# A second attention stage on 192 keys a block: corners in quarters of TensorE, a shared middle of 128 keys, a shifted copy of the values, and reordered first loads

## The chip, the cores and the metric

One core of one Trainium2 chip runs the whole program. The metric is the device time of one execution in microseconds, as the median of several runs. Before the change three runs took 1920.82, 1922.53 and 1925.12 us, a median of 1922.53.

## The reference

Two layers are added to the residual stream x, 1024 tokens of 1024 features, all in float32:

```python
def reference(x, ...):
    for i in range(DEPTH):                                  # DEPTH = 2
        if i % N_MIXERS == 0:                               # layer 0
            h = rms_norm(x, conv_norm[j])
            x = x + short_conv_mixer(h, conv_w_in[j], conv_w[j], conv_w_out[j])
        else:                                               # layer 1
            h = rms_norm(x, attn_norm[j])
            x = x + dilated_attention_mixer(h, attn_w_in[j], ...)
    return x
```

The convolution mixer is `proj = h @ w_in` with 8192 columns split into four parts, `y = b * conv3(c * u) * silu(z)`, and `y @ w_out`. The attention mixer projects h on queries, keys and values of three groups of 16 heads of 64 features each, and on a gate z. Group g cuts the 1024 tokens into 1, 4 or 16 residue classes (dilations 1, 4, 16); within a class a query attends to itself and the keys before it within a window:

```python
logits = einsum('brhnqd,brhnkd->brhnqk', qs, kb) * HEAD_DIM ** -0.5   # blocks of 128 queries,
valid = (step >= 0) & (step <= span) & (key_pos >= 0)                # 256 keys: previous and own block
logits = where(valid, logits + bias, -inf)
lse = logsumexp(logits)
out = einsum('brhnqk,brhnkd->brhnqd', exp(logits - lse), vb)
```

The window spans 128 keys of the class (`span` = 128 in each group). So query a of a block needs the keys from a positions after the start of the previous block up to itself: 129 of the 256. The three groups' outputs of a head are mixed by a softmax of their `lse`, multiplied by `silu(z)` and projected with `w_out` (`y @ w_out`).

## The kernel before, in words

**First stage, to about 1590 us.** Layer 0 and the projections of layer 1 are matmuls of 1024 features. Each float32 operand is split into a high and a low part of the type fp32r, and a product takes three matmuls (high x high, high x low, low x high; lines 368 to 370). `load_x` (from line 162) loads the first half of x in eight tiles on SyncE's queue, scales each with the norm's gain into the high part on ScalarE (line 171) and takes the low part on VectorE (line 172). Behind the first tile it loads the first weight tile in two halves (`raw_w`, line 153), each split in the same way (`split_w`, lines 158 and 159), the halves behind the first and the second x tile. `products(0, 0)` then runs over the eight x tiles for one output tile of 128 features, three matmuls for each; `products(1, 0)` does the same for the next output tile with the second weight tile, after `load_consts` and `plain_w(0, 1, 2)`. From there the large products are run by Strassen's scheme (lines 264 to 307). The queries and keys are written to DRAM as `qkd`, the values as `vd`, the gate as `zd`, one slab for each pair of heads.

**Second stage, from about 1590 us.** There are 8 pairs of heads (`hp`) and 3 groups (`g`), so 24 units, run head by head, g = 0, 1, 2. `attention(hp, g)` makes each unit's steps: four of two blocks for g = 0 and 1, two for g = 2, whose classes are 64 tokens long, so that a step has four pairs of small blocks. That is ten steps a head and 80 in all. A block of 128 queries of g = 0 and 1 is either without a predecessor (the first block of a class: one in g = 0, four in g = 1, the first four of its order) and sees its own 128 keys, or has one and sees 256 in the layout, of which 192 are computed for each half of the queries. In g = 1 the first two steps hold only blocks without, the last two only blocks with predecessor. A step has these parts, on two heads s = 0, 1 at once (one on rows 0 to 63 of the array, one on 64 to 127):

- A: scores. Line 913 is for g = 2 (quarters of the array, 64 x 64), line 927 for a block without predecessor, line 932 for a block with one: for each half h of the queries a matmul of 192 columns into a part of the bank `ps` that is 256 columns wide. The 64 columns not written hold zeros. Then VectorE adds the bias `bt`, which also carries the mask, and takes the row's minimum of the negated sum, over 256 or 128 columns (line 945), into `xs` and `nl`. There are three banks `ps`.
- E: the exponential of `xs` on ScalarE, with its row sum (line 951).
- B: transposes of `xs` into the bank `pt`, one for each 128 columns of each head (line 958), and a copy of `pt` to `pts` by VectorE (line 869) or ScalarE (line 871); `copy` decides. There are two banks `pt`.
- C: products with the values `V` into the bank `po` (line 979 for g = 0 and 1, two for a block with predecessor, which add up in the bank; line 972 for g = 2). A bank holds half a unit's output, 64 features of two heads x 512 tokens. In g = 0 and 1 the first two steps fill one of the two banks and the last two the other, and each bank is copied to `O` as soon as its second step is done (`finish`, line 994; for g = 2 both at the unit's end, line 991).

Behind a head's last step follow, at fixed distances in steps, the shares of the three groups (through DRAM), the scaling of the outputs by them on VectorE (line 1048), their sum on GpSimd (line 1051), the gate and the split into high and low part.

**Order of the work.** The order is written out by hand: iteration k runs for lags 0, 1, LC = 4, 3, 5 to 16 and last LB = 2 what the step k minus the lag has put under that lag, then the exponentials of step k, then the dense work of iteration k. So A of step k comes first, then C of step k - 4, the head's scaling and the like, then B of step k - 2. The dense work is the output projection: for two heads and one tile of 128 features x 512 tokens, six matmuls into the bank `pd` (lines 1153 to 1155), which VectorE adds to `acc` at the start of the next iteration (line 1189). It starts in step 36, and the first of it is at about 1698 us. Loads are issued on SyncE's queue at fixed distances: queries and keys `qk` and the bias `bt` six steps ahead of a unit (lines 841, 886, 888), the values two steps ahead (line 850, two transfers). `V` has its 128 tokens of a block on the partitions; a partition's 1024 numbers are ordered by feature (64 of two heads), then by the eight blocks, so that the weights of one block are read with a stride of eight.

## Time and profile before

| | before |
|---|---|
| median of 3 runs | 1922.53 us (1920.82 to 1925.12) |
| profiled execution, its own time | 1922.75 us |
| its span in the trace | 1921.0 us |
| mean granted clock of TensorE | 0.996 |
| instructions in the trace | 30176 |
| bytes moved by DMA | 253.78 MB, mean 132 GB/s |
| share of SyncE's queue (q1) and of GpSimd's (q0) of 16 DMA engines' span | 28.5% and 12.3% |
| TensorE: lines 295, 297 and 298 (Strassen) on the chain that ended last | 22% each |
| TensorE: lines 979, 958 and 932 on it | 2%, 2% and 1% |

The table reads as follows. The span is what the profiler saw between the first and the last instruction, and the execution's own time is 1.75 us more. A granted clock of 1 is full speed. The chain that ended last is the work on which the end depended, followed back from the last instruction; most of it is the first stage. In the rows of a profile, PE is TensorE, PEld its weight loads, DVE is VectorE, ACT ScalarE, POOL GpSimd and SP SyncE, whose DMA queue is SPq. A matmul on float32 operands leaves two records in the trace, so that counts of the trace are twice those of the program for lines 913 to 932, 972 and 979, but not for a transpose or for fp32r.

### The profile page before, as it was taken

The page shows a single profiled execution, that of the slowest core. Times are in us where ns is not written, and L with a number is a line of the kernel's source. Part 1 is how long each engine was busy: PE and PEld are TensorE (multiplying, and loading weights), DVE is VectorE, ACT ScalarE, POOL GpSimd, SP SyncE. Part 2 cuts the span into 40 slices and gives each one's busy share as a digit, 9 for nine tenths or more (in the row PEclk, how much of TensorE's full clock was granted, in tenths as well). Part 3 has the DMA queues.
Part 4 walks back from the last instruction along what each step waited for, and adds up shares of the span by engine and source line. Part 5 has one row for each costly group of instructions (what it writes and reads, how often), then busy time and mean ns, then how long its engine had stood idle before and what let it go on. Part 6 is the DMA issues. An engine that isn't in the chain of part 4 may idle for free.

```text
span 1921.0 us, 30176 instructions
## 1 busy us (share of the span) xinstructions
PE 1891.1 (98%) x10690; PEld 1546.8 (81%) x10690; DVE 1488.1 (77%) x2802; ACT 881.0 (46%) x2013; POOL 910.4 (47%) x841
## 2 busy tenths in 40 slices
PE   8999999999999999999999999999999999999999
PEld 6888888888888788888888888888888887777777
DVE  7966666566666746698898698869898887988896
ACT  6533333333333534454334433444344438877780
POOL 0366666666666311334545554555454552343240
PEclk9999999999999999999999999999999999899999
DMA  6222223222222656423323332333233338897842
GB/s 207 93 81 88 91 76 106 88 88 83 88 82 89 224 179 223 152 83 132 110 98 116 116 110 89 126 110 115 80 118 103 117 126 278 256 285 222 231 137 89
DMA packets 117800, 253.78 MB, mean 132 GB/s; under 512 B 18494, under 2 KB 23838, under 8 KB 117648
## 3 DMA queue, kind: packets, MB, share of 16 engines
q1 hardware_dynamic: 93280, 176.89, 28.5%
q0 software_dynamic: 24368, 74.95, 12.3%
q8 instruction: 84, 1.38, 0.3%
q14 instruction: 68, 0.56, 0.1%
HBM read 192.53 MB, written 67.64 MB: 135 GB/s over the span
## 4 chain that ended last, share of the span: by engine, by line
PE 88%; DVE 4%; DMA 4%; issue 2%; POOL 1%; ACT 1%; SPq 0%; DVEq 0%; POOLq 0%; ACTq 0%
PE pp L295 22%; PE pp L297 22%; PE pp L298 22%; PE pp L550 3%; PE pp L551 3%; PE pp L549 3%; PE po L979 2%; PE pt L958 2%; DMA nld<-nl 1%; PE pp L370 1%; PE pp L369 1%; PE pp L368 1%; PE ps L932 1%; PE pd L1153 1%; PE pd L1155 1%
## 5 line engine op out<-in xcount | busy, mean ns | idle before, releaser
L159 DVE TENSOR_TENSOR ws<-wr,ws 128x512 fp32r<-128x512 f32 x283 | 296.1, 1048 | 116.6 <-ACT ws L158 115.5
L158 ACT ACTIVATE ws<-wr 128x512 fp32r<-128x512 f32 x283 | 177.8, 630 | 366.5 <-PE pp L298 239.6
L158 ACT ACTIVATE ws<-sr 128x512 fp32r<-128x512 f32 x276 | 173.3, 630 | 340.5 <-PE pp L298 277.2
L270 POOL TENSOR_TENSOR sr<-wr 128x512 f32<-128x512 f32 x138 | 197.2, 1429 | 249.7 <-DMA wr<-in_conv_w_in 112.8
L159 DVE TENSOR_TENSOR ws<-sr,ws 128x512 fp32r<-128x512 f32 x276 | 230.8, 842 | 85.0 <-ACT ws L158 83.0
L307 DVE TENSOR_TENSOR f<-pp,f 128x512 f32<-128x512 f32 x207 | 141.6, 684 | 80.4 <-PE pp L298 73.7
L951 ACT ACTIVATE xs<-xs,nl 128x256 f32<-128x256 f32 (+2 forms) x384 | 160.5, 423 | 0.3 <-DVE nl L945 0.3
L303 ACT ACTIVATE f<-pp 128x512 f32<-128x512 f32 x231 | 134.2, 581 | 4.9 <-PE pp L298 4.8
L270 POOL TENSOR_TENSOR sr<-wr,sr 128x512 f32<-128x512 f32 x69 | 90.6, 1313 | 64.5 <-issue 54.4
L945 DVE CUSTOM_DVE_ANT_0 xs<-ps,bt 128x256 f32<-128x256 f32 (+2 forms) x384 | 102.8, 325 | 12.1 <-PE ps L932 6.2
L295 PE MATMUL pp<-blkf,ws 128*128 128x512 f32 x276 | 109.8, 398 | 0.7 <-ACT f L303 0.7
L295 PE MATMUL pp<-blka,ws 128*128 128x512 f32 x276 | 107.5, 389 | 0.7 <-ACT f L303 0.7
L297 PE MATMUL pp<-blkd,ws 128*128 128x512 f32 x276 | 107.8, 391 | 0.0
L295 PE MATMUL pp<-blkd,ws 128*128 128x512 f32 x276 | 107.7, 390 | 0.0
L295 PE MATMUL pp<-blkb,ws 128*128 128x512 f32 x276 | 107.7, 390 | 0.0
L298 PE MATMUL pp<-blkf,ws 128*128 128x512 f32 x276 | 107.7, 390 | 0.0
L297 PE MATMUL pp<-blkf,ws 128*128 128x512 f32 x276 | 107.6, 390 | 0.0
L295 PE MATMUL pp<-blkg,ws 128*128 128x512 f32 x276 | 107.6, 390 | 0.0
L295 PE MATMUL pp<-blke,ws 128*128 128x512 f32 x276 | 107.6, 390 | 0.0
L298 PE MATMUL pp<-blke,ws 128*128 128x512 f32 x276 | 107.6, 390 | 0.0
L298 PE MATMUL pp<-blkb,ws 128*128 128x512 f32 x276 | 107.4, 389 | 0.0
L297 PE MATMUL pp<-blke,ws 128*128 128x512 f32 x276 | 107.4, 389 | 0.0
(339 smaller groups left out, 5180.1 us busy)
## 6 DMA issues: line engine op xcount, KB each, us to landing
wr<-in_conv_w_in SPq DMA_DIRECT2D x128, 256.0 KB, 3.2
wr<-in_wqk SPq DMA_DIRECT2D x96, 256.0 KB, 3.4
qkd<-blkc POOLq DMA_DIRECT2D x48, 512.0 KB, 3.9
qk<-qkd SPq DMA_DIRECT2D x48, 512.0 KB, 5.4
wr<-in_conv_w_out SPq DMA_DIRECT2D x64, 256.0 KB, 3.2
f<-in_x SPq DMA_DIRECT2D x48, 256.0 KB, 4.4
wr<-in_wv SPq DMA_DIRECT2D x48, 256.0 KB, 3.2
vd<-blkc POOLq DMA_DIRECT2D x96, 128.0 KB, 2.8
```

What stands on the lines that cost most here:

```text
L158: nc.scalar.activation(t[:, 0], src, AF.Copy)
L159: nc.vector.tensor_tensor(t[:, 1], src, t[:, 0].bitcast(F32), op=OP.subtract)
L270: nc.gpsimd.tensor_tensor(t, x, y, op=op)
L295: nc.tensor.matmul(ps, w[:, 0, ws], b[:, k, 0], start=new and k == 0, stop=False, skip_group_check=not new)
L297: nc.tensor.matmul(ps, w[:, 0, ws], b[:, k, 1], start=False, stop=False, skip_group_check=not new)
L298: nc.tensor.matmul(ps, w[:, 1, ws], b[:, k, 0], start=False, stop=end and k == 3, skip_group_check=not new)
L303: nc.scalar.activation(t, ps, AF.Copy)
L307: nc.vector.tensor_tensor(m, ps, m, op=OP.add)
L549: nc.tensor.matmul(ps[dt], w[:, 0, ws], b[:, k, 0], start=(q == k == 0), stop=False)
L550: nc.tensor.matmul(ps[dt], w[:, 0, ws], b[:, k, 1], start=False, stop=False)
L945: nc.vector.tensor_tensor_reduce(out=x, in0=flat[s][:, cols], in1=u["bt"][s][:, bs], op0=OP.add, op1=OP.min, scale=-1.0, scalar=3e38, accu ...
L951: nc.scalar.activation(x, x, AF.Exp, bias=nm, scale=-1.0, accum_out=L)
```

## The change

The change touches the start of the first stage and the second stage.

**First loads.** A copy of one column on ScalarE, which needs only a constant, is put at the start, so that the table of ScalarE's functions is loaded by it. `load_x` loads four half weight tiles between the first four x tiles, two of each of the first two weight tiles, and splits each behind its x tile. `first_products` runs over the x tiles once and does the three matmuls of both output tiles for each. The third weight tile's load comes ahead of the constants.

**Scores.** The 192 keys of a block with predecessor are laid out without a gap: columns 64 to 191 are the keys from 64 before the block's start to 63 after it, which both halves of the queries need (the shared middle), and columns 0 to 63 are the keys that one half needs alone, the corner: keys -128 to -65 for the lower half of the queries, 64 to 127 for the upper. `xs` and `pts` shrink to three times 128 columns. Reductions, exponentials and copies run over 192 columns. The bias is loaded in three pieces in this layout for each head.

**Corners and ends.** `corners` transposes the corners in quarters of the array (64 x 64 matmuls with `ident`), four for a block, two into each of the banks `pt`. B transposes only the middle, one for each head. `ends` multiplies the transposed corners with the values, four 64 x 64 matmuls for a block, into the same output columns as the middle's product. Two heads and two halves of the queries make the four quarters. C has one product of 128 keys for a block and head, the middle with `W`, or for a block without predecessor its own keys with `V`.

**W.** The values are loaded a second time for g = 0 and 1, shifted by 64 tokens, so that the middle's 128 keys stand on the 128 partitions: two more transfers for each such unit, behind V's, with two buffers. Corners are taken from `V` or `W`, whichever has them on the right rows.

**Steps and banks.** In g = 1 a step now has one block without and one with predecessor ([0, 4], [1, 5], [2, 6], [3, 7]). Both output banks of a unit are taken at its first corner products, and both are copied at its last step.

**Order.** An iteration runs A of step k, `corners` of step k - 2, `ends` of step k - 4, and then B of step k - 2 if the iteration has no dense work; then lags 1, 4 (C), 3, 5 to 16 as before; and B last if it has.

```diff
+    nc.scalar.activation(consts.tile([P, 1], F32, name="warm"), ones, AF.Copy)
...
-                if hf == kt == 0:
-                    r0 = raw_w(a["conv_w_in"][0, 0], 2)
+                if hf == 0 and kt < 4:
+                    k, c = ((0, 0), (1, 0), (0, 1), (1, 1))[kt]
+                    if kt < 2:
+                        raws[k] = wq.tile([P, 1024], F32, name="wr", tag="wr", bufs=2)
+                    cs = slice(c * HALF, c * HALF + HALF)
+                    nc.sync.dma_start(raws[k][:, cs], a["conv_w_in"][0, k][:, cs])
...
-                if hf == kt == 0:
-                    W[0] = [split_w(r0[:, :HALF])]
-                if hf == 0 and kt == 1:
-                    W[0].append(split_w(r0[:, HALF:]))
+                if hf == 0 and kt < 4:
+                    W.setdefault(k, []).append(split_w(raws[k][:, cs]))
...
+            def first_products():
+                t = [cps.tile([P, HALF], F32, name="pp", tag="pp") for _ in range(2)]
+                for kt in range(KT):
+                    ws = slice(kt % 4 * P, kt % 4 * P + P)
+                    for k in range(2):
+                        w, b = W[k][kt // 4], B[kt // 4, 0]
+                        nc.tensor.matmul(t[k], w[:, 0, ws], b[:, kt % 4, 0], start=(kt == 0), stop=False)
+                        nc.tensor.matmul(t[k], w[:, 0, ws], b[:, kt % 4, 1], start=False, stop=False)
+                        nc.tensor.matmul(t[k], w[:, 1, ws], b[:, kt % 4, 0], start=False, stop=(kt == KT - 1))
+                return t
...
+                plain_w(0, 2, 2)
                 load_consts()
-                plain_w(0, 1, 2)
-                plain_w(0, 2, 2)
-                ps[0, 0] = products(0, 0)
+                ps[0, 0], ps[1, 0] = first_products()
                 load_x(1)
-                ps[1, 0] = products(1, 0)
...
+            if g < 2:
+                t = WS[hp, g] = ap.tile([P, P + 1, 8], F32, name="W", tag="W", bufs=2)
+                t = t.rearrange("p a b -> p (a b)")
+                nc.sync.dma_start(t[:64, 1:S + 1], vd[hp, g, 64:])
+                nc.sync.dma_start(t[64:, :S], vd[hp, g, :64])
...
-                        nc.sync.dma_start(b0, rows[:, :256])
+                        nc.sync.dma_start(b0[lo], rows[:64, :256])
+                        nc.sync.dma_start(b0[up, 64:], rows[64:128, 64:256])
+                        nc.sync.dma_start(b0[up, :64], rows[64:128, 192:256])
...
+                        w = P if alone else 192
+                        for h, to, at_, m in ((0, 0, 0, 64), (1, 0, 0, P)) if alone else \
+                                ((0, 0, -P, 192), (1, 64, -64, P), (1, 0, 64, 64)):
+                            for s, hs in enumerate((lo, up)):
+                                nc.tensor.matmul(flat[s][64 * h:64 * h + 64, x0 + to:x0 + to + m],
+                                                 q[hs, b * P + 64 * h:b * P + 64 * h + 64],
+                                                 k[hs, b * P + at_:b * P + at_ + m], start=True, stop=True)
+                        todo.append((slice(x0, x0 + w), j, slice(128, 256) if alone else slice(0, 192)))
+                        c.append((x0, j, b, alone))
+                        x0 += w
...
+                def corners():
+                    if g == 2:
+                        return
+                    for s in range(2):
+                        pt.append(ptp.tile([P, 4, P], F32, name="pt", tag="pt"))
+                    n = 0
+                    for i, (x0, j, b, alone) in enumerate(c):
+                        if not alone:
+                            for h, hs in enumerate((lo, up)):
+                                for s in range(2):
+                                    x = xs[s].rearrange("p a b -> p (a b)")
+                                    to = (lo, up)[s ^ i]
+                                    nc.tensor.matmul(pt[h].rearrange("p a b -> p (a b)")
+                                                     [to, 256 + 64 * n:256 + 64 * n + 64],
+                                                     x[hs, x0:x0 + 64], ident[hs, hs], start=True, stop=True)
+                            n += 1
...
+                        for i in range(len(c)):
+                            x0 = i * P if g == 2 else c[i][0] + (0 if c[i][3] else 64)
+                            nc.tensor.transpose(pt[s][:, i], x[:, x0:x0 + P], ident)
+                        pts.append(ap.tile([P, 3, P], F32, name="pts", tag="pts", bufs=6))
+                        copy(*(y.rearrange("p a b -> p (a b)")[:, :n] for y in (pts[s], pt[s])), s)
...
+                def banks_for():
+                    if js[0] == 0:
+                        for q in range(2):
+                            u["po", q] = opp.tile([P, HALF], F32, name="po", tag="po")
+                def put(i, s, hs, j, qs, w, p):
+                    po = u["po", i][hs]
+                    po = po.rearrange("p (s c) -> p c s", c=4)[:, j % 4] if g == 1 else \
+                        po[:, P * (j // 2):P * (j // 2) + P]
+                    nc.tensor.matmul(po[:, qs], w, p, start=(i, s) in first, stop=True, skip_group_check=True)
+                    first.discard((i, s))
+                def ends():
+                    if g == 2:
+                        return
+                    banks_for()
+                    V = VS[hp, g]
+                    w = WS[hp, g].rearrange("p a b -> p (a b)")
+                    for h, qs in enumerate((lo, up)):
+                        n = 256
+                        for i, (x0, j, b, alone) in enumerate(c):
+                            if not alone:
+                                for s, hs in enumerate((lo, up)):
+                                    rs = (lo, up)[s ^ i]
+                                    p = pts[h].rearrange("p a b -> p (a b)")[rs, n:n + 64]
+                                    if h == s ^ i:
+                                        put(i, s, hs, j, qs, V[rs, hs, b - 1 + h], p)
+                                    else:
+                                        b0 = 512 * s + b + (1 if h else -1)
+                                        put(i, s, hs, j, qs, w[rs, b0:b0 + 505:8], p)
+                                n += 64
...
+                                put(i, s, hs, j, slice(0, P), (V if alone else WS[hp, g])[:, hs, b], pts[s][:, i])
+                    if js[-1] == 7:
+                        for q in range(2):
                             finish(q)
...
+                           [[2 * q, 2 * q + 4], [2 * q + 1, 2 * q + 5]] if g == 1 else
...
-            for lag in (0, 1, LC, 3, *range(LC + 1, 17), LB):
-                for f in steps[k - lag].get(lag, ()) if 0 <= k - lag < len(steps) else ():
+            lags = [(0, 0), ("corners", LB), ("ends", LC)] + [(x, x) for x in (1, LC, 3, *range(LC + 1, 17))]
+            lags.insert(len(lags) if extra.get(k) else 3, (LB, LB))
+            for what, lag in lags:
+                for f in steps[k - lag].get(what, ()) if 0 <= k - lag < len(steps) else ():
```

The order of instructions shows it at three places. The first is TensorE's order in steps 7 and 8 of the first head, where the products pass from unit g = 0 to g = 1. `ps` are scores, `xs` and `pts` the exponentials before and after the transpose, `pt` the bank between, `po` an output bank. Before:

```order
L932 MATMUL ps<-qk 64x192 x8
L979 MATMUL po<-pts,V 64x128 x8
L958 MATMUL pt<-ident,xs 128x128 x4
L913 MATMUL ps<-qk 64x64 x16
L979 MATMUL po<-pts,V 64x128 x4
L958 MATMUL pt<-ident,xs 128x128 x8
```

and now:

```order
L992 MATMUL pt<-ident,xs 128x128 x4
L1007 MATMUL po<-pts,W 64x128 x4
L934 MATMUL ps<-qk 64x64 x16
L979 MATMUL pt<-ident,xs 64x64 x4
L1007 MATMUL po<-pts,W 64x64
L1007 MATMUL po<-pts,V 64x64 x2
L1007 MATMUL po<-pts,W 64x64
L992 MATMUL pt<-ident,xs 128x128 x4
L1007 MATMUL po<-pts,V 64x128 x2
L1007 MATMUL po<-pts,W 64x128 x2
```

The transposes moved ahead of the products (line 958 stood last, line 992 stands ahead of line 1007's 64x128), and behind the scores of step 8 stand four small transposes and four corner products, which are the first to write the next unit's output banks.

The second is VectorE's order at the same place; `nl` are the row minima, `o` the unit's output. Before:

```order
L945 ISA xs,nl<-ps,bt 128x256
L945 ISA nl 128x1
L994 COPY o<-po 128x512
L869 COPY pts<-pt 128x256
L945 ISA xs,nl<-ps,bt 128x64
```

and now:

```order
L959 ISA xs,nl<-ps,bt 128x192
L959 ISA nl 128x1
L888 COPY pts<-pt 128x320
L1062 COPY o<-po 128x4x128 x2
L959 ISA xs,nl<-ps,bt 128x64
```

One copy of 512 columns stood ahead of the copy of transposed scores; now both halves of the output are copied there, one behind the other, after it.

The third is SyncE's order of issues around the loads of a head's second unit. Before:

```order
L888 DMA bt<-sk_85 128x256 x2
L841 DMA qk<-qkd 128x1024 x2
L850 DMA V<-vd 128x512 x2
L886 DMA bt<-sk_86 64x64 x4
L841 DMA qk<-qkd 128x1024 x2
```

and now:

```order
L907 DMA bt<-sk_87 64x256
L908 DMA bt<-sk_87 64x192
L909 DMA bt<-sk_87 64x64
L907 DMA bt<-sk_87 64x256
L908 DMA bt<-sk_87 64x192
L909 DMA bt<-sk_87 64x64
L855 DMA qk<-qkd 128x1024 x2
L864 DMA V<-vd 128x512 x2
L869 DMA W<-vd 64x1024
L870 DMA W<-vd 64x1024
L905 DMA bt<-sk_88 64x64 x4
```

Six bias pieces stand where two stood, and the two transfers of W follow V's.

74 lines of the change are left out of this document (28 added, 46 removed).

## The prediction

> **What bounds the kernel now.** I read the totals first, then the busy time by stage, then the order of work on TensorE in the second stage, then its waits.
>
> ```profile
> PE 1891.1 (98%) x10690; PEld 1546.8 (81%) x10690; DVE 1488.1 (77%) x2802; ACT 881.0 (46%) x2013; POOL 910.4 (47%) x841
> ```
>
> The windows give TensorE, its weight loads, VectorE, ScalarE and GpSimd, then the granted clock and the DMA share:
>
> ```profile
> 0.00:46.00 46.00, 38.22 (x166) 30.20 (x167) 31.70 (x60) 30.34 (x50) 2.50 (x11) 1.00 0.60 200
> 46.00:1588.00 1542.00, 1538.99 (x6790) 1265.65 (x6789) 1172.25 (x1665) 621.34 (x1059) 811.01 (x709) 1.00 0.35 112
> 1588.00:1698.00 110.00, 99.74 (x1396) 79.59 (x1395) 96.76 (x436) 95.25 (x386) 34.33 (x44) 0.94 0.85 274
> 1698.00:1880.00 182.00, 176.96 (x2142) 140.48 (x2140) 161.13 (x600) 132.79 (x519) 62.59 (x77) 0.99 0.69 205
> 1880.00:1921.00 41.00, 37.19 (x204) 30.86 (x203) 26.24 (x44) 1.26 (x2) 0.00 (x0) 1.00 0.28 103
> ```
>
> From 46 to 1588 us TensorE idles 3 us in 1542, and the change touches nothing there: whatever is won before 46 us arrives at 1588. What is left is the first 46 us (7.8 us idle) and the second stage, 333 us. Its 80 steps fall into two kinds. To 1698 us a step is attention alone; there TensorE is idle 10.3 us and its clock averages 0.94, while VectorE works 96.8 of 110 us. From 1698 us most steps carry six matmuls of the output projection, and TensorE works 177 of 182.
>
> The timeline of TensorE shows three groups a step; the time of a group is from its start to the next start:
>
> ```profile
> 1601.33 0.71 PE L927 MATMUL ps<-qk 64*128 64x128 f32 x8
> 1601.97 1.24 PE L979 MATMUL po<-pts,V 128*64 128x128 f32 x16
> 1603.15 1.09 PE L958 MATMUL pt<-ident,xs 128*128 128x128 f32 x8
> 1604.17 0.88 PE L932 MATMUL ps<-qk 64*64 64x192 f32 x16
> ...
> 1606.75 0.88 PE L932 MATMUL ps<-qk 64*64 64x192 f32 x16
> 1607.56 1.24 PE L979 MATMUL po<-pts,V 128*64 128x128 f32 x16
> 1608.73 0.66 PE L958 MATMUL pt<-ident,xs 128*128 128x128 f32 x4
> 1609.32 0.69 PE L913 MATMUL ps<-qk 64*64 64x64 f32 x32
> 1609.94 0.76 PE L979 MATMUL po<-pts,V 128*64 128x128 f32 x8
> 1610.63 1.09 PE L958 MATMUL pt<-ident,xs 128*128 128x128 f32 x8
> ...
> 1622.45 1.07 PE L972 MATMUL po<-pts,V 64*64 64x64 f32 x32
> 1623.45 1.09 PE L958 MATMUL pt<-ident,xs 128*128 128x128 f32 x8
> ```
>
> An fp32 matmul leaves two records, a transpose one. Scores of two blocks with predecessor (x16) take 0.81 us, their eight transposes 1.02 (from 1603.15 to 1604.17), their eight products with V 1.17: 3.00 us. Two blocks without predecessor take 0.64 (1601.33 to 1601.97) + 0.59 (four transposes) + 0.69 = 1.92 us. Differences of equal groups give the slopes: (1.17-0.69)/8 = 0.06 us a record of V products and 0.21 us fixed; (1.02-0.59)/4 = 0.107 us a transpose and 0.16 fixed. The fixed part is the turn from one array shape to the next. The quarter-array groups (64\*64) take 0.62 us for 32 records at L913, 0.014 each less 0.17 fixed; at L972, with weights taken from V at a stride, 1.00 us, 0.026 each. So four quarters do run at once: 16 matmuls of 64 columns in 0.62 us.
>
> **The first 46 us.** The first activation waits for x, and its table load only starts then (SP's issues, their row in the transfers of the first 8 us with the us to landing, then ScalarE and TensorE):
>
> ```profile
> 1.65 0.90 SPq L153 DMA_DIRECT2D wr<-in_conv_w_in  x2
> ...
> wr<-in_conv_w_in SPq DMA_DIRECT2D x2, 256.0 KB, 3.9
> ...
> 3.87 1.28 ACT L171 ACT_TABLE_LOAD   x1 [3.87 <-DMA f<-in_x]
> ...
> 5.79 0.61 ACT L158 ACTIVATE ws<-wr 128x512 fp32r<-128x512 f32 x1
> ...
> 6.46 0.79 PE L368 MATMUL pp<-blka,ws 128*128 128x512 f32 x1 [6.46 <-ACT ws L158]
> ...
> 14.21 0.50 PE L369 MATMUL pp<-blkb,ws 128*128 128x512 f32 x1 [0.56 <-DVE blkb L172]
> ...
> 20.27 0.39 PE L370 MATMUL pp<-blkb,ws 128*128 128x512 f32 x1
> ```
>
> With the table in place before x lands, ScalarE could be 1.28 us earlier, but the first weights then bind: their copy cannot start before they land, 1.65 + 3.9 = 5.55 us by the first rows, and it starts at 5.79 now. So TensorE starts some 0.3 us earlier, not 1.3. The larger gain is the interleaving: each x tile now feeds six matmuls (1.4 us) where it fed three, so TensorE no longer waits tile by tile, and the 48 matmuls that end at 20.5 us should end near 18.8. The loads behind them keep their order and gain the same. Term: -1.7 us, bounds -3 and 0 (the second weight comes late and the wait is only moved).
>
> **Steps of the second stage, on TensorE.** For two blocks with predecessor: scores as many columns in 12 instructions for 8, 0.81 to 0.83 us; corners 16 records at L913's 0.014, 0.22; four transposes 0.59; corner products 16 records at L972's 0.026, 0.42 (their V and W columns have V's stride); shared products 8 records, 0.48 + 0.21 = 0.69. Scores, corners and corner products share one array shape and pay one turn, so the turns stay three a step. Sum 2.75 against 3.00: -0.25, three times a head. The middle group now pairs a block without and one with predecessor: 0.73 + 0.11 + 0.59 + (0.21 to 0.42) + 0.69 = 2.33 to 2.54 us, against the mean of 1.92 and 3.00, 2.46: four times a head -0.13 to +0.08. The open size is the corner products on two of the four quarters: 0.21 if the strided read is shared by quarters, 0.42 if each pays its own; I take the middle. The first step of a head, -0.2. Per head about -0.8, for eight heads -6.5. In the 44 steps from 1698 us on it counts in full (-3.6); before, VectorE sets part of the pace, and I take half (-1.5). Term: -5.1, bounds -12 and +1.
>
> **Waits of TensorE there:**
>
> ```profile
> PE pt L958 <- DVE pts L869: 6.3, 7, 2.5
> PE po L979 <- DVE o L991: 4.1, 5, 0.9
> ...
> PE pd L1153 <- DVE acc L1189: 2.1, 1, 2.1
> PE ps L932 <- DVE nl L945: 1.1, 2, 0.7
> ```
>
> *Unit boundaries.* Both output banks are now held from a unit's first corner product to its last step, where both are copied one behind the other, and the next unit's corner products, early in the next step, wait for both; behind them on TensorE stand the transposes, the shared products and any dense matmuls, and VectorE and ScalarE wait for these.
>
> ```profile
> L994 DVE COPY o<-po 128x512 f32<-128x512 f32 x32 | 22.0, 686 | 2.9 <-PE po L979 2.7
> ...
> L991 DVE COPY o<-po 128x512 f32<-128x512 f32 x16 | 15.2, 1022 | 0.4 <-PE po L972 0.4
> ...
> L945 DVE CUSTOM_DVE_ANT_0 xs<-ps,bt 128x256 f32<-128x256 f32 x176 | 64.8, 419 | 6.2 <-PE ps L932 3.9 <-ACT xs L951 1.6
> ...
> L945 DVE CUSTOM_DVE_ANT_0 xs<-ps,bt 128x128 f32<-128x128 f32 x80 | 19.3, 286 | 4.3 <-PE ps L932 2.3 <-ACT xs L951 1.4 <-PE ps L927 0.5
> ```
>
> Two copies of the first and second group take 1.3 us, of the third 2.0; until then TensorE has scores and corners, 0.8 us. That is 0.5 us at the first boundary and 0.2 more than now at the third, in the 4.3 heads' worth of steps without dense work: 4.3 x 0.7 = 3.0. With dense matmuls (1.5 us) between, they cover it. Term: +3.2, bounds 0 and +17 (see the rival).
>
> *Relief of VectorE and ScalarE.* A score reduction of 192 columns instead of 256 saves half of (419-286) = 67 ns, 176 times, 11.7 us of VectorE; the copies shrink by a quarter. What TensorE can get of it is in its waits (13.6 us above) and the clock after them:
>
> ```profile
> 1650.05 3.80 DVE L1048 TENSOR_TENSOR o<-o,sqacc 128x1024 f32<-128x1024 f32 x1
> 1653.78 0.54 DVE L869 COPY pts<-pt 128x384 f32<-128x384 f32 x1
> ...
> 1654.38 0.66 PE L958 MATMUL pt<-ident,xs 128*128 128x128 f32 x4 [2.52 <-DVE pts L869]
> ...
> 1658.00:1668.00 10.00, 9.46 (x78) 7.34 (x75) 8.94 (x36) 7.98 (x23) 5.01 (x9) 0.62 0.56 182
> ```
>
> A copy of transposed scores stood behind a scaling of 3.80 us; TensorE lost 2.52 us and then ran ten at 0.62 clock, 3.8 us more. In steps without dense work the copy now comes ahead of such scaling; but the next score reductions then stand behind it, and VectorE's chain there is as long as before. Term: -3, bounds -10 and 0. [...]
>
> *Loads.* W adds 0.5 MB to each of 16 units, and the bias of a head comes in three pieces instead of one.
>
> ```profile
> 1589.87 0.84 SPq L850 DMA_DIRECT2D V<-vd  x2
> ...
> 1599.38 1.00 PE L979 MATMUL po<-pts,V 128*64 128x128 f32 x12
> ...
> V<-vd SPq DMA_DIRECT2D x48, 256.0 KB, 6.5
> ```
>
> W is issued behind V on SP's queue, after 4 more bias issues (0.42 us each, as V's), and needed by the first corner products, a little before 1599.38. By the 6.5 us of V, under a DMA share near 1, it lands about 1600: +0.7 once (0 to 3). Later units have V issued some five steps ahead. The DMA share of 0.85 to 1698 us rises by 4 MB in 30: +1, bounds 0 and +6.
>
> **Sum.** -1.7 - 5.1 + 3.2 - 3 + 0.7 + 1 = -4.9 us. The profiled execution took 1922.75 us, span 1921.0 with 1.75 around it, and is 0.2 above the median 1922.53. So 1917.9, rounded 1918.0. About 0.2% (3.8 us) is what a measurement of this kernel can tell from no change; the forecast is just beyond it.
>
> **Rivals.**
> *VectorE's late copies decide (slower), 0.15.* At every one of 24 unit boundaries TensorE waits 0.9 us, today's longest, or more, since VectorE is behind with reductions when the last step ends; dense matmuls don't cover it when VectorE is 1.5 us late. 24 x 0.9 = 21.6, less the 4.1 there are: +17.5 in place of +3.2, 1932. For it: VectorE works 161 of 182 us even in the dense steps. Against: it has 12 us less to do. It decides from about 0.4 us mean wait a boundary.
> *Quarters that share a bank run one after the other, 0.06.* The corner products of one block write both halves of one bank from different row quarters; at L913 and L972 the row quarters write different banks, so no row shows this. If serial, corner products double, 0.42 x 64 steps = 27 us more: 1945. [...] No run here shows it yet.
> *No change, 0.2.* The strided reads cost 0.42 in every step and VectorE's chain hides the rest: term two -1, relief 0, boundaries +3.2: about 1922.5.
> *A larger gain, 0.2.* The long waits at heads' ends shrink below what drops the clock, and the steps gain in full: relief -9, term two -7: 1910.
>
> The forecast has 0.39; its own range is 1914 to 1922, so some two fifths of it fall within 0.2%. Faster: 0.24 + 0.2 = 0.44; same: 0.15 + 0.17 of the third = 0.32; slower 0.24. The range 1908 to 1930 leaves out the bank rival, half of the first rival and the end of the last, under 0.2.
>
> **What would show it.** Right: 48 matmuls done by 19 us; second stage without dense 2 to 4 us shorter, with dense 3 to 5; a two-predecessor step of about 2.75 us; TensorE waiting for output copies 7 us in all. Wrong: corner products above 0.6 us a step (banks or strides), waits for output copies above 15 us, waits for W, or 48 matmuls still ending at 20 us.

## The result and the profile after

The changed kernel took 1941.64 us, the median of four runs (1939.88 to 1943.38), against 1923.61 us for the kernel before in four runs: the ratio is 1.0091, with a 95% interval of 1.0078 to 1.0104. By the ratio that is slower by 17.5 us (the two medians differ by 18.0), where the prediction said 4.6 us faster and put the end of its range at 1930. The profiled execution took 1943.38 us, its span is 1941.6.

The totals and the stages, first the busy times of the page, then the windows that answer to those shown before (TensorE, its weight loads, VectorE, ScalarE, GpSimd, granted clock, DMA share, GB/s); the window to 1711 us ends at the first dense matmul, the next at the last step's scores:

```profile
PE 1899.7 (98%) x12082; PEld 1563.7 (81%) x12082; DVE 1464.5 (75%) x2802; ACT 865.8 (45%) x2014; POOL 910.0 (47%) x841
...
0.00:46.00 46.00, 38.63 (x168) 31.19 (x169) 31.88 (x60) 31.06 (x51) 2.85 (x12) 1.00 0.62 202
...
1588.00:1711.00 123.00, 103.66 (x2041) 87.31 (x2039) 87.04 (x435) 89.47 (x385) 34.27 (x44) 0.88 0.95 263
1711.00:1882.00 171.00, 163.31 (x2684) 134.09 (x2684) 142.09 (x560) 115.71 (x486) 59.15 (x75) 0.99 0.92 254
1882.00:1942.00 60.00, 55.11 (x419) 45.27 (x408) 38.21 (x83) 9.34 (x36) 3.33 (x3) 0.96 0.19 72
```

VectorE works 87 us up to the first dense matmul where it worked 96.8, as the change meant, and TensorE is not the shorter for it: it idles 19 us there, at a clock of 0.88 instead of 0.94. The column that moved the other way is the next to last: the DMA engines are busy 0.95 and 0.92 of the time, where it was 0.85 up to 1698 us and 0.75 from there to the last step's scores at 1864 us. Taking the second stage from its first scores, to the first dense matmul, to the last scores, to the last matmul's end, the profiled executions compare like this:

| stretch | before, us | after, us | difference |
|---|---|---|---|
| up to the first scores | 1591.18 | 1590.53 | -0.65 |
| to the first dense matmul | 106.95 | 121.00 | +14.05 |
| to the last step's scores | 166.04 | 170.56 | +4.5 |
| to the end of the last matmul | 53.0 | 55.7 | +2.7 |

TensorE's waits in the second stage (what waited, for whom; us in total, times, longest; "issue" is time without a wait that the profile shows):

```profile
PE ps L947 <- DVE nl L959: 9.3, 6, 5.6
PE ps L947 <- issue: 4.2, 3, 2.1
PE pd L1223 <- DVE acc L1259: 4.2, 1, 4.2
...
PE po L1007 <- DMA W<-vd: 2.1, 2, 1.2
...
PE po L1039 <- DVE o L1060: 0.6, 1, 0.6
...
PE po L1007 <- DVE o L1057: 0.3, 1, 0.3
```

The wait for output copies, 4.1 us before, is nearly gone, and so is the one for copies of transposed scores (6.3). What replaces them are a few long waits for VectorE's score reductions and for an addition to `acc`. VectorE's own waits say why they come late:

```profile
DVE xs L959 <- PE ps L947: 15.7, 16, 1.5
DVE mx L1087 <- DMA ml<-nld: 10.1, 3, 7.1
...
DVE mx L1087 <- issue: 2.3, 1, 2.3
```

`ml` are the minima and sums of a head's first two groups, written to DRAM and fetched again by GpSimd's queue, and line 1087 is the first use of them for the shares. While VectorE stands there, the reductions of the next scores stand behind it: in the longest of these waits line 1087 starts at 1698.51 us, after 7.08 us of idle time, and the next reductions follow from 1700.26, though the last of their scores ended at about 1693.2. In the chain of waits one of these places reads as follows (start, us, what):

```profile
1669.70 5.18 DMA fd<-fo
...
1678.66 11.83 DMA nld<-nl
...
1691.31 7.08 DMA ml<-nld
...
1698.51 0.19 DVE mx L1087
```

A store of 16 KB was 11.83 us on its way and the fetch behind it 7.08, and TensorE at the same place:

```profile
1694.94 0.42 PE L947 MATMUL ps<-qk 64*64 64x64 f32 x2
1700.95 1.12 PE L947 MATMUL ps<-qk 64*64 64x64 f32 x14 [5.59 <-DVE nl L959]
```

These look like transfers that wait among others. In the transfers of the second stage up to 1865 us (KB each, median us from issue to landing) `ml` went from 4.8 to 7.1 us, `fb`, the shares fetched for the scaling, from 7.0 to 9.2:

```profile
W<-vd SPq DMA_DIRECT2D x32, 256.0 KB, 7.6
fb<-fd POOLq DMA_DIRECT2D x24, 256.0 KB, 9.2
...
ml<-nld POOLq DMA_DIRECT2D x28, 8.0 KB, 7.1
```

### The profile page after: what moved, and what is told of

Its sections match the earlier page's. It is cut to its first block, busy times and chain, and to the rows that moved or that the text cites. A ratio compares the mean times of both kernels' runs of the same rounds, so it can differ in the third digit from the quotient of the medians.

```text
span 1941.6 us, 33113 instructions
## 1 busy us (share of the span) xinstructions
PE 1899.7 (98%) x12082; PEld 1563.7 (81%) x12082; DVE 1464.5 (75%) x2802; ACT 865.8 (45%) x2014; POOL 910.0 (47%) x841
## 3 DMA queue, kind: packets, MB, share of 16 engines
q0 software_dynamic: 24368, 74.95, 11.9%
## 4 chain that ended last, share of the span: by engine, by line
PE 84%; DMA 5%; DVE 3%; issue 2%; POOL 1%; SPq 0%; ACT 0%; DVEq 0%; POOLq 0%
PE pp L299 22%; PE pp L301 21%; PE pp L302 21%; PE pp L564 3%; PE pp L565 3%; PE pp L563 3%; PE po L1007 2%; DMA nld<-nl 1%; PE pt L992 1%; DMA W<-vd 1%; PE ps L947 1%; PE pd L1223 1%; PE pd L1225 1%; PE pd L1224 1%; DMA ml<-nld 1%
## 5 line engine op out<-in xcount | busy, mean ns | idle before, releaser
L160 DVE TENSOR_TENSOR ws<-wr,ws 128x512 fp32r<-128x512 f32 x283 | 285.1, 1009 | 116.1 <-ACT ws L159 115.1
L965 ACT ACTIVATE xs<-xs,nl 128x192 f32<-128x192 f32 (+2 forms) x384 | 151.1, 399 | 2.1 <-DVE nl L959 2.1
L299 PE MATMUL pp<-blkf,ws 128*128 128x512 f32 x276 | 109.8, 398 | 0.7 <-ACT f L307 0.7
L959 DVE CUSTOM_DVE_ANT_0 xs<-ps,bt 128x192 f32<-128x192 f32 (+2 forms) x384 | 90.8, 295 | 22.5 <-PE ps L947 15.7
L299 PE MATMUL pp<-blkg,ws 128*128 128x512 f32 x276 | 107.6, 390 | 0.0
L302 PE MATMUL pp<-blkf,ws 128*128 128x512 f32 x276 | 107.4, 389 | 0.0
L302 PE MATMUL pp<-blkg,ws 128*128 128x512 f32 x276 | 107.4, 389 | 0.0
```

What stands on the lines that cost most here:

```text
L160: nc.vector.tensor_tensor(t[:, 1], src, t[:, 0].bitcast(F32), op=OP.subtract)
L299: nc.tensor.matmul(ps, w[:, 0, ws], b[:, k, 0], start=new and k == 0, stop=False, skip_group_check=not new)
L302: nc.tensor.matmul(ps, w[:, 1, ws], b[:, k, 0], start=False, stop=end and k == 3, skip_group_check=not new)
L959: nc.vector.tensor_tensor_reduce(out=x, in0=flat[s][:, cols], in1=u["bt"][s][:, bs], op0=OP.add, op1=OP.min, scale=-1.0, scalar=3e38, accu ...
L965: nc.scalar.activation(x, x, AF.Exp, bias=nm, scale=-1.0, accum_out=L)
```

## The experiments

The theory after this reading, D: W's transfers fill the DMA engines, the small transfers that carry the shares come late, and VectorE and TensorE wait behind them. The rivals were Q, that the quarters of the array cost TensorE more than they save, and O, that the new order or the output copies at a unit's end cost it. Fourteen kernels were run; the ratio is always to the kernel before, with the 95% interval.

| run | what it is | ratio | interval |
|---|---|---|---|
| the change | | 1.0091 | 1.0078 to 1.0104 |
| e1_no_w | without W's transfers | 1.0017 | 1.0006 to 1.0029 |
| e2_before_traffic | before, with W's bytes moved in DRAM | 1.0017 | 1.0006 to 1.0027 |
| e3_w_aligned | W not 4 bytes off | 1.0122 | 1.0102 to 1.0143 |
| e4_b_last | transposes always last | 1.0127 | 1.0109 to 1.0146 |
| e5_start_only | before, with the new first loads | 0.9987 | 0.9979 to 0.9995 |
| e6_late_weights | first use of `ml` later | 1.0113 | 1.0100 to 1.0126 |
| e7_w_v_form | W in V's form of transfer | 1.0064 | 1.0050 to 1.0078 |
| e8_no_w_dense_read | e1, corner weights without stride | 1.0010 | 0.9999 to 1.0020 |
| e9_no_w_whole_bias | e1, bias in one transfer | 1.0016 | 1.0006 to 1.0026 |
| e10_w_unread | W loaded, not read | 1.0122 | 1.0097 to 1.0147 |
| e11_w_on_gpsimd | W copied from V by GpSimd | 1.0107 | 1.0092 to 1.0122 |
| e12_w_on_act | W copied from V by ScalarE | 1.0065 | 1.0050 to 1.0080 |
| e13_start_and_order | before, new first loads and order | 0.9986 | 0.9976 to 0.9995 |
| e14_start_order_all | the same, order in every iteration | 1.0042 | 1.0029 to 1.0056 |

**Without W's transfers.**

```diff
-                t = WS[hp, g] = ap.tile([P, P + 1, 8], F32, name="W", tag="W", bufs=2)
-                t = t.rearrange("p a b -> p (a b)")
-                nc.sync.dma_start(t[:64, 1:S + 1], vd[hp, g, 64:])
-                nc.sync.dma_start(t[64:, :S], vd[hp, g, :64])
+                WS[hp, g] = VS[hp, g]
...
-                                        b0 = 512 * s + b + (1 if h else -1)
+                                        b0 = 512 * s + b
```

> The changed kernel without W's two transfers a unit; it reads V where it read W, so that its output is not the reference's. Theory D (the DMA engines are full: W and the bias pieces delay the small transfers of the shares, VectorE stands waiting for ml in program order, and TensorE idles and loses clock behind it): of the 18 us lost most comes back, 1920 to 1927 us, DMA share before the first dense step back from 0.96 to about 0.85, waits of VectorE for ml back from 12 us to under 4. Rival Q (scores, corners and corner products in quarters of the array cost TensorE more than they save): no more than 4 us come back, 1937 to 1942. Rival O (the order of transposes and the two output copies at a unit's end): the same, 1937 to 1942.

Measured: 1926.86 us, ratio 1.0017. Its windows, to the first dense matmul and to the last scores, and VectorE's wait for `ml`:

```profile
1588.00:1699.00 111.00, 100.91 (x2042) 85.06 (x2042) 85.92 (x434) 89.08 (x385) 36.44 (x49) 0.94 0.86 269
1699.00:1865.00 166.00, 161.12 (x2684) 132.44 (x2686) 141.77 (x559) 116.06 (x487) 55.38 (x69) 1.00 0.80 226
...
DVE mx L1084 <- DMA ml<-nld: 2.9, 1, 2.9
```

The DMA share falls back to 0.86, the clock returns to 0.94, the wait for `ml` from 10.1 to 2.9 us, and 0.74% (14 us) of the loss is gone: Q and O had it within 4 us of the changed kernel. W is the larger part. Not every transfer is early again: `ml` lands in 5.8 us here (7.1 with W, 4.8 before), but `fb` still takes 8.9 (9.2 and 7.0), so its lateness is not W's.

**W loaded, not read**, to tell its traffic from the wait for it.

```diff
-                    w = WS[hp, g].rearrange("p a b -> p (a b)")
+                    w = V.rearrange("p a b -> p (a b)")
...
-                                put(i, s, hs, j, slice(0, P), (V if alone else WS[hp, g])[:, hs, b], pts[s][:, i])
+                                put(i, s, hs, j, slice(0, P), V[:, hs, b], pts[s][:, i])
```

> The changed kernel with W loaded in full but read by nobody (products and corners read V, wrong values). If W costs by its traffic: 1938 to 1943, ratio 1.0075 to 1.010, as with W read. If it costs by the wait of the first corner products for it and by what stands behind that on TensorE: ratio 1.001 to 1.004, near the kernel without W's transfers.

Measured: ratio 1.0122, no faster than with W read, though nobody waits for W. So it is the traffic. But its way to the time is another here: VectorE has no wait for `ml`, which lands in 5.1 us, and TensorE's largest wait is for the queries and keys themselves:

```profile
PE ps L947 <- DMA qk<-qkd: 10.4, 4, 5.3
```

So the part of theory D that says which transfer is late does not hold in general; that W's traffic costs the time does.

**The same bytes on the kernel before.** The bytes go from `vd` to a place in DRAM (`more`) that nobody reads.

```diff
+        more = dram.tile([HP, 2, 2, 64, S], F32, name="more")
...
+            if g < 2:
+                for i in range(2):
+                    nc.sync.dma_start(more[hp, g, i], vd[hp, g, 64 * i:64 * i + 64])
```

> The kernel before plus W's bytes: behind V's transfers of each unit of the first two groups two transfers of 64 rows of 4 KB from vd to a place in DRAM that nobody reads. D: slower by 8 to 20 us, 1931 to 1943, with VectorE waiting for ml. Q and O: within 2 us of before, 1922 to 1926.

Measured: 1927.55 us, ratio 1.0017: slower by 3 us, not by 8 to 20. D as put here fell: the bytes alone do not cost what W costs. VectorE's wait for `ml` did rise, from 1.3 to 6.3 us in two places.

**The form of W's transfers.** The next run loads W as V is loaded, 128 rows of 2 KB a transfer instead of 64 rows of 4 KB.

```diff
-                nc.sync.dma_start(t[:64, 1:S + 1], vd[hp, g, 64:])
-                nc.sync.dma_start(t[64:, :S], vd[hp, g, :64])
+                for q in range(2):
+                    nc.sync.dma_start(t[:, half(q)], vd[hp, g, :, half(q)])
...
-                                        b0 = 512 * s + b + (1 if h else -1)
+                                        b0 = 512 * s + b
```

> The changed kernel with W loaded in the form of V: two transfers of 128 rows of 2 KB instead of two of 64 rows of 4 KB, not shifted (its products take wrong values, the work is the same). If it is the form (64 partitions at a time) that makes W dear, 47 us of 16 engines' time for 8.4 MB where V's form costs about half: DMA share before the first dense step falls from 0.96 to 0.91, and 6 to 12 us come back, 1930 to 1936. If it is the bytes: within 3 us of 1942.

Measured: ratio 1.0064, so 5 of the 17.5 us come back, a little less than the 6 to 12 of the first theory. The pages' rows for SyncE's queue (packets, MB, share of 16 engines' span) say what W took of the engines, for the changed kernel, without W, and in V's form:

```profile
q1 hardware_dynamic: 98912, 185.29, 30.7%
```

```profile
q1 hardware_dynamic: 96352, 176.90, 28.7%
```

```profile
q1 hardware_dynamic: 100960, 185.29, 29.9%
```

Times the spans (1941.6, 1926.1 and 1933.6 us) these are 596, 553 and 578 us of 16 engines: the same 8.4 MB took 43 us in transfers of 64 partitions and 25 us in transfers of 128. The sizes are rough, for the same row differs by some 10 us between kernels that should not differ in it: 593 to 605 us in the five that load W in 64 partitions, 545 to 554 in the four that do not load it and keep the bias in pieces. With the means of these, 598.5 and 550.6, the prices are 47.9 and 27.6, the same ratio of 1.7. The copy within DRAM, of the same rows of 4 KB, took 25 us too (29.8% of 1922.6, against 28.5% of 1921.0), so the row's length alone does not make the price. Why the transfers of 64 partitions are the dearer ones no run shows. Nor does the form explain the 0.47% by which V's form (1.0064) is still above the kernel without W (1.0017). The prediction did not weigh the form of the transfers.

**W four bytes off.**

```diff
-                nc.sync.dma_start(t[:64, 1:S + 1], vd[hp, g, 64:])
+                nc.sync.dma_start(t[:64, :S], vd[hp, g, 64:])
...
-                                        b0 = 512 * s + b + (1 if h else -1)
+                                        b0 = 512 * s + b
```

> The changed kernel with W's first transfer written at column 0 instead of 1 (its products then take wrong values, the work is the same). If the transfers of W are dear because their rows start 4 bytes off, W's landing falls from 7.6 us to V's 6.4 and some 5 to 12 us come back, 1930 to 1937. If it is the bytes alone: within 2 us of 1941.6. Q and O: within 2 us of 1941.6.

Measured: ratio 1.0122, no gain. The offset of the rows is not the cause. The work is that of the change, and yet the ratio is 0.3% above the change's; the kernels with W's transfers in this form lie between 1.0091 and 1.0127 here, so a difference of 0.3% between two of them says little, and W's price is 14 us or somewhat more.

**The first use of `ml` later.**

```diff
-                    w, v, y = {0: (3, 11, 14), 1: (4, 11, 14), 2: (3, 10, 13)}.get(hp, (2, 9, 13))
+                    w, v, y = {0: (5, 11, 14), 1: (5, 11, 14), 2: (4, 10, 13)}.get(hp, (3, 9, 13))
```

> The changed kernel with VectorE's first use of the fetched ml (the weights of the three groups) two steps later in the first head, one step later in the others, and the shares and their spreading with it; scalings where they were. Theory D1 (VectorE's wait for ml in program order is what turns full DMA engines into lost TensorE time): the waits for ml go from 12 us to under 5 and 5 to 10 us come back, 1932 to 1937, unless the scalings now wait for fb instead. Rival D2 (the lost time is spread over all transfers, so that the next wait, for fb or for bt and W, takes the place of this one): 1939 to 1944, with waits of VectorE for fb above 8 us.

Measured: ratio 1.0113. VectorE's waits:

```profile
DVE o L1117 <- DMA fb<-fd: 13.9, 5, 4.3
...
DVE mx L1087 <- DMA ml<-nld: 5.0, 3, 2.3
```

The wait for `ml` was halved and the next, for `fb` (2.1 us in the changed kernel), took its place, as D2 had it, though 1946.31 us lies 2 above its range. In this run there was no single wait to move away.

**W made on the chip**, by GpSimd, then by ScalarE, from V, one and two iterations into the unit.

```diff
-                nc.sync.dma_start(t[:64, 1:S + 1], vd[hp, g, 64:])
-                nc.sync.dma_start(t[64:, :S], vd[hp, g, :64])
...
+                nc.gpsimd.tensor_copy(t[:64, 1:S + 1], v[64:])
...
+                nc.gpsimd.tensor_copy(t[64:, :S], v[:64])
...
+            if un[1] < 2:
+                when(k + 1, shift, un, 0)
+                when(k + 2, shift, un, 1)
```

ScalarE's run has `nc.scalar.activation(..., AF.Copy)` in both places.

> The changed kernel with W made on the chip: two copies of 64 partitions x 1024 columns by GpSimd from V, one and two iterations into the unit, instead of two transfers. D: the DMA share falls back as without W's transfers and most of the loss returns, ratio 1.002 to 1.005, less what the copies (some 3 us each by GpSimd's 1.43 us for 128 x 512) hold up in GpSimd's own queue, where the shares' small transfers are issued. If those are held up: 1.006 or more.

> The same with ScalarE making the two copies, about 1.1 us each by its 0.58 us for 512 columns. GpSimd's queue stays free; ScalarE works 87 of 117 us before the first dense step and has exponentials and copies of transposed scores behind these copies: ratio 1.002 to 1.006. If ScalarE is the tighter engine there: above 1.006.

Measured: 1.0107 and 1.0065. GpSimd's copies took 1.13 us (the first of the two) and 1.04 (the second) in the mean, not 3, but TensorE waited 10 us for them, and GpSimd itself 14.1 us for V in four places; ScalarE's took 1.06 us each and TensorE waited for the copies of transposed scores behind them:

```profile
PE pt L983 <- ACT pts L894: 8.9, 8, 4.6
PE ps L951 <- DVE nl L963: 4.4, 6, 1.3
```

The second is faster than the changed kernel by some 5 us and still slower than before.

**The bias in one transfer**, on the kernel without W's transfers.

```diff
-                        nc.sync.dma_start(b0[lo], rows[:64, :256])
-                        nc.sync.dma_start(b0[up, 64:], rows[64:128, 64:256])
-                        nc.sync.dma_start(b0[up, :64], rows[64:128, 192:256])
+                        nc.sync.dma_start(b0, rows[:, :256])
```

> The changed kernel without W's transfers (V read in its place) and with each head's bias in one transfer of 256 columns, as before the change (the columns do not fit the new layout, so values are wrong, the work is the same). With the bias pieces the kernel without W's transfers took 1.0017 of before. If the small bias pieces have a price of their own (four more issues a unit, 6 us to landing each): 2 to 4 us less, ratio 0.9995 to 1.0007. If it is W alone: ratio 1.001 to 1.002.

Measured: 1.0016 against 1.0017. The pieces cost nothing that can be measured.

**The corner products' reads**, also without W's transfers.

```diff
-                                        put(i, s, hs, j, qs, V[rs, hs, b - 1 + h], p)
+                                        put(i, s, hs, j, qs, w[rs, 512 * s:512 * s + 64], p)
...
-                                        put(i, s, hs, j, qs, w[rs, b0:b0 + 505:8], p)
+                                        put(i, s, hs, j, qs, w[rs, 512 * s + 64:512 * s + 128], p)
```

> The changed kernel without W's transfers, as above, and with the corner products' weights read from 64 columns that lie one behind the other instead of at a stride of eight (wrong values, same work). If the strided read is what makes eight records of corner products cost 0.6 us where the prediction put 0.2 to 0.4: about 0.25 us less in each of the 64 steps, of which 42 are dense and gain in full: 1915 to 1921. If it is that two of four quarters wait for each other whatever the read: within 2 us of the same without this edit, 1925 to 1929.

Measured: ratio 1.0010. TensorE's timeline without this edit, corner products (line 1004, 64\*64) of two blocks (x15, one record stands apart) and of one block (x8), each with the transposes behind it:

```profile
1607.78 0.69 PE L1004 MATMUL po<-pts,V 64*64 64x64 f32 x15
1608.40 0.66 PE L989 MATMUL pt<-ident,xs 128*128 128x128 f32 x4
...
1617.84 0.66 PE L1004 MATMUL po<-pts,V 64*64 64x64 f32 x8
1618.43 0.66 PE L989 MATMUL pt<-ident,xs 128*128 128x128 f32 x4
```

and with it:

```profile
1606.94 0.45 PE L1004 MATMUL po<-pts,V 64*64 64x64 f32 x15
1607.32 0.66 PE L989 MATMUL pt<-ident,xs 128*128 128x128 f32 x4
...
1616.73 0.42 PE L1004 MATMUL po<-pts,V 64*64 64x64 f32 x8
1617.08 0.65 PE L989 MATMUL pt<-ident,xs 128*128 128x128 f32 x4
```

One block's corner products take 0.59 us with the stride and 0.35 without, and two blocks' take 0.62 and 0.38. So the stride costs 0.24 us a group, as the first theory of this run said, and the time of the kernel hardly shows it: 64 groups make 15 us less work on TensorE, and the run is 0.07% (1.3 us) faster, inside the interval. Neither theory of this run had that. It is not that the steps did not get shorter. The same iteration with dense work, from scores to scores, first without this edit and then with it, took 3.96 and 3.72 us:

```profile
1716.23 0.90 PE L944 MATMUL ps<-qk 64*64 64x192 f32 x24
...
1720.19 0.90 PE L944 MATMUL ps<-qk 64*64 64x192 f32 x24
```

```profile
1719.52 0.90 PE L944 MATMUL ps<-qk 64*64 64x192 f32 x24
...
1723.24 0.90 PE L944 MATMUL ps<-qk 64*64 64x192 f32 x24
```

Every iteration with corner products that nothing delays follows in full in this way, and other iterations, longer by several us, gave the gain back: the stretch from the first scores to the first dense matmul took 112.7 us, against 108.9 without this edit. The profiled execution of this run was its slowest, 6 us above the median, so which waits took the gain back in the others is not shown.

**Transposes always last.**

```diff
-            lags.insert(len(lags) if extra.get(k) else 3, (LB, LB))
+            lags.append((LB, LB))
```

> The changed kernel with the transposes of step k - 2 always last in the iteration, as before the change. O: 5 us or more come back, 1930 to 1937, in the steps without dense work. D: within 4 us of 1941.6 either way, since the waits for ml stay. Q: within 3 us of 1941.6.

Measured: ratio 1.0127, above the change by 0.36% and above the ranges of all three theories. The wait for copies of transposed scores is back, larger than in the kernel before:

```profile
PE pt L979 <- DVE pts L888: 14.0, 10, 3.2
```

So what O said of the order fell: nothing comes back without it. That the order is a gain can't be said, since the kernel that only moved W by four bytes stands at 1.0122 with the new order. What O said of the output copies no run took apart.

**The first loads alone.** The edit is, on the kernel before, the parts of the change's diff that stand ahead of W:

```diff
+    nc.scalar.activation(consts.tile([P, 1], F32, name="warm"), ones, AF.Copy)
...
-                ps[0, 0] = products(0, 0)
+                ps[0, 0], ps[1, 0] = first_products()
```

> The kernel before with the reordered first loads and the early table load alone. By the changed kernel's profile the second stage starts 0.65 us earlier, and nothing else is touched: 0.5 to 1.0 us faster than before, which is inside what the comparison can tell. A rival that the first loads delay something later (the third weight tile, the constants) would give 0 or slower by up to 1 us. The prediction's term was -1.7.

Measured: ratio 0.9987 (0.9979 to 0.9995), about 2.5 us faster (1.0 to 4.0), near the prediction's -1.7 and more than the 0.5 to 1.0 expected from the changed kernel's profile.

**The first loads and the order on the old second stage.**

```diff
-            for lag in (0, 1, LC, 3, *range(LC + 1, 17), LB):
+            rest = (1, LC, 3, *range(LC + 1, 17))
+            for lag in (0, *rest, LB) if extra.get(k) else (0, LB, *rest):
```

> The kernel before with the reordered first loads and with the transposes of step k - 2 right behind the scores of step k in iterations without dense work; the second stage is otherwise the old one. If the order gains there too (the copy of transposed scores no longer stands behind a scaling of 3.8 us): ratio 0.995 to 0.998 against 0.9987 with the first loads alone. If the order only helps the changed kernel's corners: 0.998 to 0.9995. If it costs (the products and the output copies come later): above 0.9995, and part of the 6 us is its price.

Measured: 1919.58 us, ratio 0.9986: the fastest of all here, with the order adding nothing that can be told from the first loads alone. TensorE's waits moved instead of going away: those for copies of transposed scores fell from 5.9 us (first loads alone) to 1.2, those for score reductions rose from 1.1 to 7.3. That is what the prediction said of VectorE's chain, that the reductions would then stand behind the scaling.

```diff
-            for lag in (0, 1, LC, 3, *range(LC + 1, 17), LB):
+            for lag in (0, LB, 1, LC, 3, *range(LC + 1, 17)):
```

> The same with that order in every iteration, with dense work too. There the dense matmuls cover the copies either way, and the copies of transposed scores come earlier on VectorE than the scalings: within 0.0015 of the run above. If instead the transposes then wait for exponentials that are not done: slower than the run above by 0.002 or more.

Measured: ratio 1.0042, 0.56% slower than the run above, and for neither of the reasons given. An iteration with dense work (from scores to scores, 4.16 us):

```profile
1797.34 0.88 PE L946 MATMUL ps<-qk 64*64 64x192 f32 x16
1798.15 0.66 PE L972 MATMUL pt<-ident,xs 128*128 128x128 f32 x4
1798.73 1.24 PE L993 MATMUL po<-pts,V 128*64 128x128 f32 x16
1799.91 0.50 PE L1167 MATMUL pd<-y,y 128*128 128x512 f32 x1
...
1801.50 0.88 PE L946 MATMUL ps<-qk 64*64 64x192 f32 x16
```

Before the change such an iteration (scores, products, transposes, dense) took 3.95 us. The transposes and the dense matmuls have the same array shape, and the old order put them side by side; this one has a turn more. The four transposes take 0.58 us here, where ahead of dense matmuls they took 0.42 before (1760.62 to 1761.04 us). That is 0.2 us in each of 36 iterations, 7 us of the 11. So work put on TensorE in these iterations showed in the time.

## Why the prediction was wrong

**The direction.** The step that failed is "Loads": +1 for W's 0.5 MB a unit and +0.7 for its first arrival, bounds 0 and +6, and 0 to +3. The runs put W's transfers at 0.74% of the time, 14 us, so this term was mis-sized by more than its bounds. The prediction read that the DMA share was 0.85 and that 4 MB in 30 would be added, and left it at +1: it priced W by V's bytes. Two things were missed. In transfers of 64 partitions W took some 43 us of the engines, not the 25 that V's form takes. And with the share at 0.95 other transfers became the waits. In the changed kernel's trace it is `ml`, at the end of a chain of four trips through DRAM in each head, for which VectorE waits in its order; in the run with W unread it is the queries and keys, and in the one with the later use of `ml` it is `fb`. That W's traffic costs the time is shown; that it does so by one certain transfer is not. The prediction looked at where W itself is needed and found it hidden, which was right (2.1 us of waits), and did not ask who else uses the engines that W fills.

By the runs the 17.5 us are about -2.5 for the first loads, +6 for the rest of the change without W's transfers, and +14 for these. So without W's transfers the kernel would still have been slower (1.0017), inside the prediction's range and not the way it forecast: the gains of "Steps" and "Relief" did not come either.

**Step work: -5.1, measured about 0.** The clean iterations show it. From 1698 us on, those of a head's ten iterations whose neighbours all had dense work take, at the median, 4.05, 4.23, 3.96, 3.96, 3.73 and 3.74 us before and 3.85, 4.08, 3.98, 3.97, 3.86 and 3.89 after, 23.67 and 23.63 in sum. (The prediction's own sum has a slip here: 3 x 0.25, 4 x 0.025 and 0.2 are 1.05 us a head, not 0.8, which would make the term -6.5; likewise 4.3 x 0.7 at the unit boundaries is 3.0, not 3.2. Neither changes the direction.) A timeline of the changed kernel, an iteration without dense work and without waits:

```profile
1619.37 0.90 PE L947 MATMUL ps<-qk 64*64 64x192 f32 x24
1620.07 0.22 PE L1007 MATMUL po<-pts,W 64*64 64x64 f32 x1
...
1620.66 0.66 PE L992 MATMUL pt<-ident,xs 128*128 128x128 f32 x4
1621.25 0.51 PE L1007 MATMUL po<-pts,V 128*64 128x128 f32 x4
...
1621.94 0.90 PE L947 MATMUL ps<-qk 64*64 64x192 f32 x24
```

Scores took 0.70 us (predicted 0.82), transposes 0.59 and shared products 0.69 as predicted, and the corner products of one block, where the prediction took the middle of 0.21 and 0.42, took 0.59. The stride makes 0.24 of it, which is as much as the prediction wanted to save in a step. The prediction's 0.42, each quarter paying for its own strided read, and some 0.17 that looks like a turn of its own, which it had let the corner products share with the scores, would give the 0.59. The range given, "0.21 if the strided read is shared by quarters, 0.42 if each pays its own", ended too low.

**Even so the sum was not the point.** The run with the reads made cheap shows that 15 us less work on TensorE moved the time by 1. The prediction counted the dense steps in full, because TensorE works 177 of 182 us there. Undelayed steps did follow in full, but waits in other steps grew by as much. Whether they grow because the other engines are nearly as busy (VectorE 161 of 182 us) is not shown.

**Relief: -3, measured a loss.** The size of the relief was right: each of the 176 reductions of a block with predecessor takes 353 ns instead of 419, 66 ns less where the prediction had 67, 11.6 us in all:

```profile
L959 DVE CUSTOM_DVE_ANT_0 xs<-ps,bt 128x192 f32<-128x192 f32 x176 | 56.7, 353 | 6.0 <-PE ps L947 5.3 <-ACT f L1091 0.6
```

In the changed kernel's trace it did not reach TensorE: VectorE stood 10.1 + 2.3 us for `ml`, and up to the first dense matmul, with 19 us of TensorE's idle time, the clock was 0.88 (0.94 before), where the prediction had it rise. Without W's transfers the clock is 0.94 as before the change, so it did not rise there either.

**Unit boundaries: +3.2, measured -3.6**: TensorE's waits for output copies fell from 4.1 + 0.4 to 0.3 + 0.6 us. So the rival of VectorE's late copies, which also had the kernel slower, had the sign and not the cause; its waits did not come. **The rival of banks run one after the other**, whose 1945 is close to the time measured, fell too: the corner products of two blocks, in two banks, take 0.62 us and those of one block 0.59, and without the stride 0.35 for eight records in one bank. By an estimate from L913's 0.014 us a record with four quarters at work, a record alone takes four times as long, 0.056: one after the other the eight would take 8 x 0.056 + 0.17 = 0.62, two at once 0.39.

**The start: -1.7, measured about -2.5.** The number was near, and that was partly luck, for the path was another. TensorE started at 6.11 us instead of 6.46, as predicted, but the 48 matmuls ended at 20.2 and not by 19, one of the prediction's own signs of being wrong. In the trace of the first loads alone only 0.6 us is won when the 48 are done, and 2.2 at the end of the first stage; where the rest comes from is open. The late end has to do with TensorE's pace: one matmul in 0.43 us until 11.8 us (0.23 from then on), where before the change it was until 10.3. A wait of 0.5 us behind the first three is not enough to explain it, since with the first loads alone there is no such wait and the pace changed at 11.9 all the same.

**What stays open.** Without W's transfers the second stage is still 0.3% (some 6 us) slower than the old one with the same first loads. The order alone on the old steps and the bias are not it. In the profiled executions some 3 us of it lie between the first scores and the first dense matmul (108.9 against 105.8 us); whether it is the pairing of blocks in the second group, the corners' hold on the `pt` banks or both output copies at the unit's end was not tried apart. No run explains the last stretch, 2.7 us longer in the changed kernel's profile at a clock of 0.96. It is also open why W in V's form still costs 9 us, where the same use of the engines cost the old kernel 3, or what decides which waits W's traffic lengthens, since they differ from run to run.

## What to carry to other kernels

A second copy of data that "arrives in time" was not free here, where the DMA engines were already busy 0.85 of the time: its transfers cost 14 us. List the other transfers on which an engine waits in its order, and ask what becomes of their landing times. The form counted beside the bytes: loaded over all 128 partitions instead of in two halves of 64, the copy here (then not shifted) cost 5 us less, and still 9. And before TensorE's groups are shortened, make one of them cheap in a run and see whether the time of the whole kernel follows, and not only that of the step.

## What the runs showed of the hardware

**VectorE and GpSimd.** In the changed kernel's trace the scaling by `fb` took 1.22 us each of 14 times. That by `sqacc`, of the same shape, took 1.22 us once and 1.36 to 3.65 the other six times, and in these six an addition on GpSimd ran beside it. The longest:

```profile
1732.04 3.65 DVE L1117 TENSOR_TENSOR o<-o,sqacc 128x1024 f32<-128x1024 f32 x1
```

```profile
1732.21 2.38 POOL L1120 TENSOR_TENSOR o<-o 128x1024 f32<-128x1024 f32 x1
```

The addition ended at 1734.59 us and the scaling at 1735.69, 1.10 later. In all six the scaling ends 1.09 to 1.10 us after the addition, however much of the addition was left at its start: it looks as if the scaling did its work only when the addition was done. The addition took 2.37 or 2.38 us each time. That it waited for the addition is an estimate from these six places: no run took the addition away. The scaling of 3.80 us that the prediction read before the change has such an addition beside it too: that one ran from 1650.39 us for 2.37, and the scaling, from 1650.05 on, ended 1.09 after it.

**A transfer of 64 partitions took 1.7 times the engine time of one of 128** for the same bytes (43 against 25 us for 8.4 MB, rows of 4 and of 2 KB), above. **A stride of eight in TensorE's weights cost 0.24 us a group** of eight or sixteen 64 x 64 records, above.
